# Two conventional FFN tiles put into the seven-product form at the start of the last block

## The chip, the cores and the metric

The kernel runs on one core of one Trainium2 chip. The metric is the time on the device in microseconds of one execution; lower is better. Before the change the median of three runs is 2493.28 us (2493.01 to 2493.83). The core has five engines with queues of their own: PE (TensorE, matrix products into PSUM), DVE (VectorE), ACT (ScalarE), POOL (GpSimd) and SP (SyncE, which here issues the DMAs). PEld in the profile is PE's loading of the stationary operand.

## The reference

Two pre-norm residual layers over a sequence of 1024 tokens, `D_MODEL` 1024, all in float32. The first has a Mamba-2 mixer, the second a Conformer convolution module; each mixer is followed by a SwiGLU feed-forward network (FFN) with `D_FF` 2816, that is 22 tiles of 128; a final RMSNorm ends the stack. What matters here is the second layer's FFN and the end:

```
def swiglu_ffn(u, w_gate, w_up, w_down):
    return (jax.nn.silu(u @ w_gate) * (u @ w_up)) @ w_down
...
        h = h + swiglu_ffn(rmsnorm(h, ffn_norm[i]), ffn_w_gate[i], ffn_w_up[i], ffn_w_down[i])
    return rmsnorm(h, final_norm)
```

## The kernel before

**Data.** The tokens lie in two blocks of 512 (block 0 and block 1). Activations are kept transposed: `h` has eight tiles of 128 features by 512 tokens for each block. Float32 accuracy comes from splitting each operand into an upper and a lower part (`split`, line 233: ACT copies the upper part, line 234, and DVE subtracts, line 235), and from three matmuls for each product: low by high, high by low, high by high (`gemm`, line 255).

**The FFN** of a block takes its 22 tiles in parts. For each part the gate and up products fill `hid`, and then eight output products (`dn`, line 977), one for each 128 output features, add the part's share to `h` (line 985). A conventional tile (`gu`, line 938) takes 24 matmuls of 512 columns for gate and 24 for up; its weights are split from `wst` into `whi` and `wlo`.

**The seven-product form** (`seven`, line 832) computes two neighbouring tiles at once by Strassen's scheme in Winograd's variant: the two tiles, the two halves of the features and the two halves (256 tokens) of the block make a 2 by 2 product of blocks that takes seven products instead of eight. Each product is 12 matmuls of 256 columns (line 881). It needs sums of the weights (`sums`, lines 850 to 852, on DVE), splits of the weights (`wa`, `wb`, `wc`) and readbacks of single products (lines 892 to 917). Gate and up of a pair are two such halves. On the other side it needs sums of the normalized input u: `sums_u` (line 783), whose three steps make t2 (`first`, lines 811 to 813 and a split), n3 and t4 (`second`, line 819 and two splits), and one operand written over a part of u (`last`, line 825). For block 1 of the last layer `norm_u` (line 324, `whole=True`) also leaves the unsplit u in `ru`, from which these sums start.

**The order.** Work is cut into units, and `run` makes a list `q` of them. Each unit's instructions get their priority from their place in the list; the scheduler below the kernel then sets each engine's own order from the priorities and what is ready in its reckoning. `chain7` (line 1009 on) strings the seven-product units of several parts together and puts one output product behind at least `gap` of them, from `lag` units after the part before is done; the last part's output products end the chain. So the first part of a chain has none of its own chain between its products. If the first part is conventional (a list of units, not of dictionaries), its units come first. Fetches, weight sums and weight splits are put ahead by `emit`: `pre` (line 921) gives how many us ahead of its unit each is to come, in times that the kernel reckons itself (`MM`, `MH`), and they get a priority earlier by `BOOST`. `put` and `at` insert units at given positions of a list, negative ones counted from its end.

**The place of the change.** At the end of `run` the last layer's block 0 runs tiles 12 to 21 in the seven-product form, with block 1's norm (`n1`) inserted near its end: five units, before the last ten to five units of the chain. The last eight units of that chain are the output products of block 0's last part of six tiles. Then comes block 1: tiles 0 and 1 conventional, then parts of 6, 6, 4 and 4 tiles in the seven-product form; the sums of u stand after the first, second and fourth conventional unit, and the final norm of block 0 (`f0`: one unit, then four that scale and store) after the second and third. The last part (tiles 18 to 21) has its output products in halves of 256 tokens, between which the final norm of block 1 runs (`f1`, `f2`).

Of the kernel before, what the change touches and what calls it, by code (L numbers as in the profile page):

```python
# [73 lines left out]
class Unit:  # L74
# [3 lines left out]
    def __init__(self, run, load=None, t=0.0, pre=()):  # L78
        self.run, self.load, self.t, self.pre, self.then = run, load, t, pre, None


def weave(main, fill):

    out, n, m, j = [], len(main), len(fill), 0
    for i, f in enumerate(main):
        out.append(f)
        want = (i + 1) * m // n
        out += fill[j:want]
        j = want
    return out  # L90


def put(q, *at):

    out = []
    for i in range(len(q) + 1):
        for k, units in at:
            if (k if k >= 0 else len(q) + k) == i:
                out += units
        out += q[i:i + 1]  # L100
    return out


def at(units, places):

    return [(p, units[i:i + 1] if i < len(places) - 1 else units[i:]) for i, p in enumerate(places)]


class Trunk:
# [405 lines left out]
    def in_proj(self, i, u=None, fac=None):  # L515
# [12 lines left out]
        def run(n):  # L528
# [9 lines left out]
            else:  # L538
# [3 lines left out]
                self.nc.scalar.activation(s, acc, AF.Tanh, scale=0.5)  # L542
                self.nc.vector.scalar_tensor_tensor(s, s, 1.0, acc, op0=ALU.add, op1=ALU.mult)
        units = [Unit(lambda n=n: run(n), lambda n=n: load(n)) for n in range(10)]
        if u is not None:
            self.W_in = W
# [649 lines left out]
    def run(self):  # L1196
        nc = self.nc
        self.h = {0: [], 1: []}
        self.U, self.UB, self.TU, self.TB, self.RU, self.sums, self.LU, self.LB = ({} for _ in range(8))
        self.whole = set()  # L1200
        self.ci, self.co = [], {0: [], 1: []}
        call = lambda f, *a: Unit(lambda: f(*a))
        self.consts()
        self.mixer_setup()
        fac = self.small.new("fac")
        raw = []
        dt = self.dt_path(0, raw, fac)
        r3, ip = self.in_proj(0, raw, fac)
        self.banks(mm=(0, 1, 2, 3, 4, 5), ss=(6, 7))
        self.warm(WARM)  # L1210
        products, rb = self.begin(raw, dt[0].load)
        r3[0].load()
        r3[0].load = None
        nu = self.norm_u(0, "ssm_norm", 0, fac, (0, 1, 3, 5, 7))
        q = [products] + nu[:2] + [call(self.halves, fac)] + nu[2:] + r3 + [call(lambda: self.big.drop(*rb))]
        q += dt[1:2] + [call(self.selects)] + dt[2:] + ip[:NR]
        q += [call(lambda: self.small.drop(fac)), call(lambda: self.banks(mm=(0, 1, 2, 3), ss=(4, 5, 6, 7)))] + ip[NR:]
        q += [call(self.load_x, 1)]
        for i in range(8):
            wo = self.w_out(i - 1) if i else []  # L1220
            post = []
            if i == 3:
                dtp = self.dt_path(1)
                ip = self.in_proj(4)
                n1 = self.norm_u(1, "ssm_norm")
                fill = [self.drop_u(0)] + put(wo, *at(n1, (0, 2, 3, 4, 6))) + dtp[:1] + ip[:1] + dtp[1:2] + ip[1:]
                post = dtp[2:]
            elif i < 7:
                ip = self.in_proj(i + 1)
                fill = ip[:3] + wo + ip[3:]  # L1230
                if i == 2:
                    fill = put(fill, *at(self.x_sums(1), range(1, 17, 2)))
            else:
                ag, ad = self.ffn(0, 18, 4, [0])
                fill = [self.drop_u(1)] + put(wo, *at(self.norm_u(0, "ffn_norm"), (2, 4, 5, 6, 8))) + ag[:6]
            q += weave(self.ssd(i), fill) + post
        q += [Unit(lambda: (self.big.drop(*self.mix_bigs), self.half.drop(*self.c_er, self.c_xt))), call(self.phase, 8)]
        fast = lambda *a, **k: self.ffn(*a, fast=True, **k)
        su = self.sums_u(0)
        q += ag[6:] + put(weave(self.w_out(7), ad), *at(su, (1, 3, 5, 8, 16)))  # L1240
        n1 = self.norm_u(1, "ffn_norm")
        c = self.chain7(fast(0, 0, 6, [0]), fast(0, 6, 6, [0]), fast(0, 12, 6, [0], [0]), free=0, hold=0)
        q += [call(self.phase7)] + put(c, *at(n1, (-10, -8, -7, -6, -5))) + [call(self.phase, 8)]
        n0 = self.norm_u(0, "cv_norm")
        p1, cv = self.pw1(0), self.conv31(0, 1000)
        c = self.chain(self.ffn(0, 10, 6, [1]), self.ffn(0, 16, 6, [1]))
        q += put(c[:4], *at(n0, (0, 1))) + [call(self.phase, 6, nc.gpsimd)]
        for j in range(8):
            q += p1[2 * j:2 * j + 2] + (cv[j:j + 1] if j < 4 else [])
        ln, p2 = self.cnorm(0), self.pw2(0)  # L1250
        q += cv[4:] + put(c[4:], *at(ln, (-11, -10, -9, -7, -5, -4, -3, -2)))
        q += [call(self.phase, 8)]
        q += put(p2, *at(self.sums_u(1, True), (2, 3, 4, 5, 6)))
        n0 = self.norm_u(0, "ffn_norm", 8)
        c = self.chain7(fast(0, 0, 4, [1]), fast(0, 4, 6, [1], [1]), free=1, hold=0)
        q += [call(self.phase7)] + put(c, *at(n0, (-10, -8, -7, -6, -5))) + [call(self.phase, 8)]
        n1 = self.norm_u(1, "cv_norm")
        p1, cv = self.pw1(1), self.conv31(1, 1200)
        c = self.chain(self.ffn(1, 0, 6, [0]), self.ffn(1, 6, 6, [0]))
        q += put(c[:4], *at(n1, (0, 1))) + [call(self.phase, 6, nc.gpsimd)]  # L1260
        for j in range(8):
            q += p1[2 * j:2 * j + 2] + (cv[j:j + 1] if j < 4 else [])
        ln, p2 = self.cnorm(1), self.pw2(1)
        q += cv[4:] + put(c[4:], *at(ln, (-11, -10, -9, -7, -5, -4, -3, -2)))
        q += [call(self.phase, 8)]
        self.whole = {1}
        q += put(p2, *at(self.sums_u(0, True), (2, 3, 4, 5, 6)))
        n1 = self.norm_u(1, "ffn_norm", 8, whole=True)
        c = self.chain7(fast(1, 12, 4, [0]), fast(1, 16, 6, [0], [0]), free=0, hold=0)
        q += [call(self.phase7)] + put(c, *at(n1, (-10, -8, -7, -6, -5)))  # L1270
        f0, f1, f2 = self.final(0), self.final(1, (0,)), self.final(1, (HT,))
        c = self.chain7(self.ffn(1, 0, 2, [1]), fast(1, 2, 6, [1]), fast(1, 8, 6, [1]), fast(1, 14, 4, [1]),
                        fast(1, 18, 4, [1], [1], True), free=1, hold=4)
        q += put(c, *at(self.sums_u(1), (1, 2, 4)), (2, f0[:1]), (3, f0[1:]), *at(f1, (-7, -5, -4, -3, -2))) + f2
        self.emit(q)

    def phase7(self):
# [100 lines left out]
```

## Time and profile before

| | |
|---|---|
| median of three runs | 2493.28 us |
| the profiled execution, its time | 2493.91 us |
| its span, first to last instruction | 2492.2 us |
| mean granted TensorE clock | 0.997 |
| block 1's norm, first to last DVE operation | 2103.3 to 2129.3 us |
| block 1's first conventional matmul | 2137.5 us |
| its first seven-product matmul | 2160.2 us |

Times in the views count from the start of the span. A row of the timeline gives start, duration, engine, line, operation, what is written from what (tile names without buffer numbers), shape, a count where equal neighbours are merged, and in brackets how long the engine was idle before and what ended that. A row of the stretches gives the stretch, its length, and for each engine its busy time and number of instructions, then the granted clock and the DMA figures. Matmuls overlap, so their durations are longer than the time from one start to the next.

### The profile page before, as it was taken

How to read it: one execution, taken by the hardware profiler on the slowest of the kernel's cores; microseconds unless marked ns; L12 is line 12 of the kernel's file. 1: busy time of each engine (PE TensorE's matmuls, PEld its weight loads, DVE VectorE, ACT ScalarE, POOL GpSimd, SP SyncE). 2: the span in 40 equal slices, each digit the busy share in tenths (PEclk: the TensorE clock that was granted, in tenths of full speed). 3: DMA queues.
4: the chain of work that ended last, by engine and by line, in shares of the span. 5: the costliest groups of instructions: out<-in, count | busy, mean ns of one | idle time of the engine just before them, and what ended most of it. 6: DMA issues, size and time to landing. Idle time of an engine off the chain costs nothing.

```text
span 2492.2 us, 35811 instructions
## 1 busy us (share of the span) xinstructions
PE 2471.1 (99%) x13752; PEld 2114.9 (85%) x13752; DVE 2052.9 (82%) x3030; ACT 1328.7 (53%) x2365; POOL 398.8 (16%) x406
## 2 busy tenths in 40 slices
PE   8999999999999999999999999999999999999998
PEld 6788887888887899998888789988887899899998
DVE  7988989878889886768799797778997977986675
ACT  5776776766667553545333455453335545554444
POOL 1212111112111000000444410004444100000000
PEclk9999999999999999999999999999999999999999
DMA  4222222222223332323223233232232323332322
GB/s 159 68 68 85 77 62 85 77 73 79 76 70 110 89 112 92 110 67 100 93 93 111 87 114 109 64 102 93 93 119 85 123 91 104 131 118 82 119 85 73
DMA packets 69516, 233.54 MB, mean 94 GB/s; under 512 B 7648, under 2 KB 11232, under 8 KB 61920
## 3 DMA queue, kind: packets, MB, share of 16 engines
q1 hardware_dynamic: 69344, 231.25, 28.5%
q8 instruction: 108, 1.77, 0.3%
q14 instruction: 64, 0.52, 0.1%
HBM read 227.02 MB, written 4.19 MB: 93 GB/s over the span
## 4 chain that ended last, share of the span: by engine, by line
PE 97%; DVE 2%; ACT 1%; issue 0%; DMA 0%; DVEq 0%; SPq 0%; ACTq 0%
PE p L259 68%; PE p L881 23%; PE p L712 1%; PE p L704 1%; PE p L667 1%; PE p L680 1%; PE p L681 1%; PE p L310 0%; PE p L647 0%; PE p L695 0%; DVE wlo L235 0%; PE p L408 0%; PE p L614 0%; PE p L615 0%; PE p L618 0%; DVE un_s L349 0%
## 5 line engine op out<-in xcount | busy, mean ns | idle before, releaser
L234 ACT ACTIVATE whi<-wst 128x512 fp32r<-128x512 f32 (+1 forms) x652 | 388.0, 597 | 689.3 <-PE p L259 577.9
L259 PE MATMUL p<-uhi_b,wlo 128*128 128x512 f32 x1344 | 533.7, 397 | 3.3 <-ACT uhi_b L234 1.8
L259 PE MATMUL p<-ulo_b,whi 128*128 128x512 f32 x1344 | 529.4, 394 | 1.6 <-POOL ulo_b L235 1.1
L259 PE MATMUL p<-uhi_b,whi 128*128 128x512 f32 x1344 | 530.5, 395 | 0.0
L259 PE MATMUL p<-hid_b,whi 128*128 128x512 f32 x1344 | 419.1, 394 | 0.2
L235 DVE TENSOR_TENSOR wlo<-wst,whi 128x512 fp32r<-128x512 f32 (+1 forms) x442 | 303.9, 690 | 123.5 <-ACT whi L234 120.2
L235 POOL TENSOR_TENSOR wlo<-wst,whi 128x512 fp32r<-128x512 f32 x208 | 256.4, 1236 | 724.3 <-ACT whi L234 720.9
L881 PE MATMUL p<-uhi_b,wh_b 128*128 128x256 f32 x1856 | 343.9, 280 | 0.0
L259 PEld LDWEIGHTS p<-uhi_b,wlo 128*128 128x128 f32 x1344 | 253.0, 188 | 62.4 <-ACT uhi_b L234 2.6
L259 PEld LDWEIGHTS p<-ulo_b,whi 128*128 128x128 f32 x1344 | 253.3, 188 | 61.9 <-POOL ulo_b L235 2.9
L259 PEld LDWEIGHTS p<-uhi_b,whi 128*128 128x128 f32 x1344 | 253.1, 188 | 59.2 <-issue 0.3
L259 PEld LDWEIGHTS p<-hid_b,whi 128*128 128x128 f32 x1344 | 251.9, 188 | 56.7 <-DVE hid_b L235 1.1
L881 PEld LDWEIGHTS p<-uhi_b,wh_b 128*128 128x128 f32 x1856 | 290.9, 188 | 3.2 <-ACT vw_s L908 0.8
L259 PE MATMUL p<-hid_b,wlo 128*128 128x512 f32 x672 | 264.3, 394 | 0.0
L881 PE MATMUL p<-ulo_b,wh_b 128*128 128x256 f32 x928 | 259.9, 280 | 0.0
L881 PE MATMUL p<-tu_b,wh_b 128*128 128x256 f32 x1392 | 183.2, 281 | 0.0
L881 PEld LDWEIGHTS p<-ulo_b,wh_b 128*128 128x128 f32 x928 | 174.6, 188 | 2.0
L234 ACT ACTIVATE wh_b<-ws_b 128x1024 fp32r<-128x1024 f32 x116 | 122.7, 1059 | 99.2 <-PE p L881 38.9
L881 PEld LDWEIGHTS p<-tu_b,wh_b 128*128 128x128 f32 x1392 | 173.6, 188 | 1.3
L1097 DVE SCALAR_TENSOR_TENSOR p<-ci_b,par,p 128x507 f32<-128x507 f32 (+29 forms) x240 | 160.3, 733 | 3.3 <-ACT p L1094 2.0
L235 DVE TENSOR_TENSOR wh_b<-ws_b,wh_b 128x1024 fp32r<-128x1024 f32 x116 | 141.1, 1221 | 25.6 <-ACT wh_b L234 25.3
L1099 DVE SCALAR_TENSOR_TENSOR p<-ci_b,par,p 128x512 f32<-128x512 f32 x232 | 158.1, 749 | 1.9 <-ACT p L1094 1.4
(282 smaller groups left out, 4027.1 us busy)
## 6 DMA issues: line engine op xcount, KB each, us to landing
wq_b<-w_gu SPq DMA_DIRECT2D x58, 1024.0 KB, 4.8
wst<-w_in SPq DMA_DIRECT2D x77, 512.0 KB, 3.5
wst<-w_dn SPq DMA_DIRECT2D x88, 384.0 KB, 3.1
wst<-w_gu SPq DMA_DIRECT2D x60, 512.0 KB, 3.5
wst<-w_pw SPq DMA_DIRECT2D x48, 512.0 KB, 3.5
wst<-w_out SPq DMA_DIRECT2D x64, 256.0 KB, 2.6
wst<-w_dn SPq DMA_DIRECT2D x40, 256.0 KB, 2.7
h<-xT SPq DMA_DIRECT2D x8, 512.0 KB, 8.8
```

What stands on the lines that cost most here:

```text
L234: self.nc.scalar.activation(hi, src, AF.Copy)
L235: (eng or self.nc.vector).tensor_tensor(lo, src, hi.bitcast(F32), ALU.subtract)
L259: self.nc.tensor.matmul(acc, a, b, start=n == 0, stop=n == tot - 1)
L667: nc.tensor.transpose(xt[:, zs(j)], self.XS[i][:, j, zs(z)], self.ident)
L680: nc.tensor.matmul(sg, self.gtr, aml, start=True, stop=False)
L681: nc.tensor.matmul(sg, self.gtr, amh, start=False, stop=True)
L704: nc.tensor.matmul(O[:, zs(j)], H[:, zs(j)], CT[:, zs(z)], start=True, stop=True)
L712: nc.tensor.matmul(Y[po:po + 64, zs(hh // 2)], self.XDT[z % 2][:, hh * 64:(hh + 1) * 64], E[:, zs(r)], start=True, stop=True)
L881: nc.tensor.matmul(to, x, y, start=n == 0 and not more, stop=n == 11, skip_group_check=True)
L1097: nc.vector.scalar_tensor_tensor(acc[:, s:], x[:, HALO:TW - s], w(s), acc[:, s:], op0=ALU.mult, op1=ALU.add)
L1099: nc.vector.scalar_tensor_tensor(acc if s < 30 else c, x[:, HALO - s:TW - s], w(s), acc, op0=ALU.mult, op1=ALU.add)
```

## The change

Block 1 of the last layer takes all 22 tiles in the seven-product form, in parts of 6, 6, 6 and 4. The three units of `sums_u(1)` move out of block 1's chain into the end of block 0's chain, before the last four, three and two units, among block 0's last output products; the units of block 1's norm after its first move up by one place each. The final norm of block 0 keeps its positions (after the second and the third unit) in block 1's chain, whose units are other ones now. The last part of four tiles is as before; the part ahead of it has six tiles instead of four.

```diff
-        q += [call(self.phase7)] + put(c, *at(n1, (-10, -8, -7, -6, -5)))
+        su = self.sums_u(1)
+        q += [call(self.phase7)] + put(c, *at(n1, (-10, -9, -8, -7, -6)), *at(su, (-4, -3, -2)))
         f0, f1, f2 = self.final(0), self.final(1, (0,)), self.final(1, (HT,))
-        c = self.chain7(self.ffn(1, 0, 2, [1]), fast(1, 2, 6, [1]), fast(1, 8, 6, [1]), fast(1, 14, 4, [1]),
+        c = self.chain7(fast(1, 0, 6, [1]), fast(1, 6, 6, [1]), fast(1, 12, 6, [1]),
                         fast(1, 18, 4, [1], [1], True), free=1, hold=4)
-        q += put(c, *at(self.sums_u(1), (1, 2, 4)), (2, f0[:1]), (3, f0[1:]), *at(f1, (-7, -5, -4, -3, -2))) + f2
+        q += put(c, (2, f0[:1]), (3, f0[1:]), *at(f1, (-7, -5, -4, -3, -2))) + f2
```

## The prediction

> **What bounds the kernel now.** I read the page first (busy shares, chain of work that ended last), then a table of stretches around the place that changes, then the timeline of PE and of DVE there.
>
> ```profile
> span 2492.2 us, 35811 instructions
> ...
> PE 2471.1 (99%) x13752; PEld 2114.9 (85%) x13752; DVE 2052.9 (82%) x3030; ACT 1328.7 (53%) x2365; POOL 398.8 (16%) x406
> ...
> PE 97%; DVE 2%; ACT 1%; issue 0%; DMA 0%; DVEq 0%; SPq 0%; ACTq 0%
> ```
>
> PE sets the end over nearly the whole span: removing PE work gains its own time, if nothing else comes late. What could come late is named by the stretches. Columns: stretch, length, then busy time (and instructions) of PE, PEld, DVE, ACT, POOL, then granted clock, DMA share and GB/s.
>
> ```profile
> 2090.00:2100.00 10.00, 10.00 (x87) 10.00 (x87) 3.10 (x5) 3.77 (x7) 0.00 (x0) 1.00 0.13 39
> 2103.30:2137.50 34.20, 34.20 (x152) 27.66 (x152) 33.08 (x54) 18.50 (x35) 0.00 (x0) 1.00 0.47 152
> 2137.50:2159.80 22.30, 22.30 (x98) 18.11 (x97) 21.80 (x29) 18.07 (x25) 0.00 (x0) 1.00 0.14 42
> 2159.80:2211.00 51.20, 51.20 (x385) 48.62 (x384) 49.75 (x73) 27.06 (x44) 0.00 (x0) 1.00 0.44 152
> 2211.00:2480.00 269.00, 269.00 (x1912) 252.34 (x1911) 190.20 (x279) 126.72 (x207) 0.00 (x0) 1.00 0.28 93
> ```
>
> The second stretch is the output products of block 0's last part, the third the two conventional tiles that are to go, the fourth the first seven-product tiles. PE has no gap in them; but DVE is busy 33.08 of 34.20, 21.80 of 22.30 and 49.75 of 51.20 us. From 2103 to 2211 DVE has 3 us to spare in 108. Whether the change gains is decided there.
>
> **What PE saves.**
>
> ```profile
> 2137.53 0.40 PE L259 MATMUL p<-uhi_b,wlo 128*128 128x512 f32 x1
> 2154.17 0.40 PE L310 MATMUL p<-suml_s,onesr 128*128 128x512 f32 x1
> 2154.40 0.39 PE L310 MATMUL p<-sumh_s,onesr 128*128 128x512 f32 x1
> 2160.18 0.28 PE L881 MATMUL p<-uhi_b,wh_b 128*128 128x256 f32 x1
> 2005.99 1.58 PE L881 MATMUL p<-tu_b,wh_b 128*128 128x256 f32 x12
> 2007.40 0.28 PE L881 MATMUL p<-uhi_b,wh_b 128*128 128x256 f32 x1
> ```
>
> The conventional tiles take 2160.18 - 2137.53 = 22.65 us; two matmuls in it are block 0's final norm (0.23 each, from one start to the next), so their 96 matmuls take 22.19. As one seven-product pair they are 14 products of 12 matmuls; a product takes 2007.40 - 2005.99 = 1.41, together 19.74. PE saves 2.45 us. The output products keep their matmuls (22 tiles by three by eight, regrouped). Eight `h += acc` on DVE disappear (40 become 32), as do eight small weight loads in w_dn; they lie after 2160 where PE does not wait, so I count them nothing. Bytes stay; four loads of 512 KB become two of 1024 KB.
>
> **What DVE must do, and by when.** Prices are taken from one start to the next in a stretch without gaps:
>
> ```profile
> 2151.86 1.22 DVE L235 TENSOR_TENSOR wh_b<-wq_b,wh_b 128x1024 fp32r<-128x1024 f32 x1
> 2153.00 0.41 DVE L235 TENSOR_TENSOR wlo<-wst,whi 128x256 fp32r<-128x256 f32 x1
> 2153.33 2.35 DVE L235 TENSOR_TENSOR wh_b<-ws_b,wh_b 128x1024 fp32r<-128x1024 f32 x2
> 2155.60 0.68 DVE L235 TENSOR_TENSOR wlo<-wq_b,whi 128x512 fp32r<-128x512 f32 x1
> 2156.20 1.22 DVE L235 TENSOR_TENSOR wh_b<-wq_b,wh_b 128x1024 fp32r<-128x1024 f32 x1
> 2105.32 0.95 DVE L967 TENSOR_TENSOR hx_x<-hx_x,hx_x 128x768 f32<-128x768 f32 x1
> 2106.19 0.69 DVE L317 SCALAR_TENSOR_TENSOR p<-p,rstd_s 128x512 f32<-128x512 f32 x1
> 2162.33 5.35 DVE L1189 SCALAR_TENSOR_TENSOR h<-h,par,p 128x512 f32<-128x512 f32 x8
> 2167.60 0.68 DVE L950 TENSOR_TENSOR sg_s<-sg_s,p 128x512 f32<-128x512 f32 x1
> ```
>
> 1024 columns 1.14, 768 columns 0.87, 512 columns 0.60, 256 columns 0.33; the eight scalar_tensor_tensor 5.27 / 8 = 0.66 each. So a gate or up half of a pair costs: weight sums (lines 850 to 852) 1.14 + 0.60 + 0.60 = 2.34, splits a11/a12, s2/s3, s1/s4 1.14 each and a22 0.60.
>
> Where does DVE stand when PE ends block 0?
>
> ```profile
> 2103.32 0.69 DVE L315 SCALAR_TENSOR_TENSOR p<-p,rstd_s 128x512 f32<-128x512 f32 x1
> 2128.61 0.69 DVE L235 TENSOR_TENSOR ulo_b<-ru_b,uhi_b 128x512 fp32r<-128x512 f32 x1
> 2136.07 1.22 DVE L812 TENSOR_TENSOR ru_b<-ru_b,ru_b 128x1024 f32<-128x1024 f32 x1
> 2139.65 1.22 DVE L813 SCALAR_TENSOR_TENSOR ru_b<-ru_b,ru_b 128x1024 f32<-128x1024 f32 x1
> 2140.78 0.68 DVE L283 TENSOR_TENSOR ssum_s<-ssum_s,sq_s 128x512 f32<-128x512 f32 x1
> 2160.25 1.23 DVE L235 TENSOR_TENSOR ulo_b<-ru_b,uhi_b 128x1024 fp32r<-128x1024 f32 x1
> ```
>
> Block 1's norm begins on DVE at 2103.3 and ends at 2129.3; of the sums of u only two of eight wide operations are done by T0 = 2137.5, the last at 2161.5. In the old order that was early enough: the seven products began at T0 + 22.7. In the new order they begin at T0.
>
> Demand counted from 2103.3, in the order in which products need it. Up to the third product (p6, needs t2 and s2): end of block 0's last pair 0.33 + 0.87 + 1.14 = 2.3; three rstd steps 1.9; norm 8 x (0.66 + 0.60) = 10.1; down weights 6 x (0.60 + 0.33) + 0.33 = 5.9; eight adds to h 4.8; seven additions of squares 4.2; lines 811 to 813 and the t2 split 4 x 1.14 = 4.6; weight sums and two splits 4.6. Sum 38.4. DVE has 34.2 until T0 and 2.8 for two products, 37.0: **1.4 us late**. (The old order's part of this, without the last 7.6 us and with three conventional splits of 0.60, is 32.6; the stretch shows 33.08.)
>
> Up to the up half's p5 (the twelfth product, due at 34.2 + 11 x 1.41 = 49.7): n3, t4 and the last split 4 x 1.14 = 4.6; the gate half's s1/s4 and a22 1.7; the up half 2.34 + 3.42 + 0.60 = 6.3; four readbacks of products into hx 4 x 0.33 = 1.3; the split for the final norm 0.6. Sum 38.4 + 14.5 = 52.9: **3.2 late**.
>
> Then the final norm of block 0, which the queue still places after the second and third unit of this chain, now two products instead of two 5.5 us units: 1.9 + 5.3 = 7.2. In the rows above its eight operations run in one piece and line 950 waits behind them, so they are taken ahead of younger work. Next gate half: a11/a12, sums, s2/s3 4.6 and a readback 0.3. Sum 65.0 for its p6, the sixteenth product, due at 34.2 + 15 x 1.41 = 55.3: **9.7 late**. Later DVE needs about 17 of each 19.7 us, so it falls no further behind. Nothing can cover on PE: block 0's output products are over, and block 1 has none until its first six tiles end, whereas before the small part's output products stood between the first products. Everything behind the late product waits in PE's queue. Block 0's output DMAs move forward on SP's queue with the norm; weights are fetched 12 us ahead of use by the queue's own reckoning (line 921), so I price that at nothing; with that cover gone, a load would be late by as much as DVE is, which is already in the sum. ACT makes the upper half of each split and was busy 18.07 of 22.30 us in the stretch that goes; the added pair gives it no more than DVE has, so it follows DVE.
>
> So the sums will not run beside block 0's output products: DVE is full there with the norm. The net is -2.45 + 9.7 = +7.3 us. The profiled execution took 2493.91 us (span 2492.2); the runs' median, 2493.28, is 0.63 lower. From it: **2500.6 us**.
>
> **Rivals.** *DVE keeps up (not slower).* Before 2103.3 DVE is mostly idle (3.10 of 10 us busy from 2090). The norm waits for two matmuls with ones at 2100.6, whose inputs are older:
>
> ```profile
> 2083.16 0.68 DVE L235 TENSOR_TENSOR suml_s<-ssum_s,sumh_s 128x512 fp32r<-128x512 f32 x1
> 2100.82 0.40 PE L310 MATMUL p<-sumh_s,onesr 128*128 128x512 f32 x1
> 2102.54 0.69 ACT L314 ACTIVATE rstd_s<-p,eps 128x512 f32<-128x512 f32 x1
> ```
>
> The change places the norm one unit earlier. If that moved those matmuls to 2091 or before, DVE would gain the 9.7 us that it lacks, and only PE's 2.45 would be left: 2490.8. Against it: one product is 1.41 us, and the matmuls already ran ahead of their place.
>
> *The final norm comes late.* If the order lets all weight work pass it, only 3.2 us are lost: 2493.28 - 2.45 + 3.2 = 2494.0. For it: it needs block 0's last squares, which finish after T0. Against: the uninterrupted eight above.
>
> *The accumulators add to it.* A third half reuses the first half's two banks, and its second product (fourteenth, due at 34.2 + 13 x 1.41 = 52.5) needs line 917 to have read the old one; if that waits behind all 65.0 us of older and prefetched work, PE pauses 12.5: 2503.3. A pause can cost clock too:
>
> ```profile
> 60.00:70.00 10.00, 5.25 (x19) 3.81 (x20) 9.35 (x15) 8.60 (x21) 4.79 (x7) 0.70 0.28 100
> 65.04 0.80 PE L680 MATMUL p<-am_b,sr_b 128*128 128x512 f32 x1 [3.12 <-ACT am_b L663]
> 70.08 0.63 PE L259 MATMUL p<-uhi_b,whi 128*128 128x512 f32 x1
> 70.51 0.58 PE L259 MATMUL p<-uhi_b,wlo 128*128 128x512 f32 x1
> ```
>
> After a pause of 3.12 us the stretch has clock 0.70 and matmuls start 0.43 apart instead of 0.23; eight such are 1.6 us. I take nothing for it in the sum, since DVE delivers an operand every 1 to 3 us, and 1.6 at the range's end: 2504.9. The Trainium skill ("TensorE: Matmul & The Clock Gate", Part 1, "What's actually happening") says the clock halves after an idle window of about 3.4 us and returns after as much busy time. By that rule one pause as long as the eight operations would cost about 1.7 us once (an estimate from the page); the row above agrees in size.
>
> **How the numbers follow.** Pause 7.5 to 11.3 us (2498.3 to 2502.1): 0.46. Accumulators or clock on top: 0.18. Final norm late, wholly or partly (2493.5 to 2498.3): 0.22. DVE keeps up (near 2490.8): 0.11. Something gained besides, below 2488.3: 0.03. About 0.2%, 5 us, is what a measurement can tell from no change. Slower 0.64, same 0.33, faster 0.03. The range, 2493.5 to 2504.9, leaves out DVE keeping up and the far ends.
>
> **What would show it.** Right: PE less than fully busy in the 25 us after T0, its idle time ended by DVE (tu, wh, hx) or by ACT halves of those splits; line 825's split ending 5 us or more after T0; DVE full from 2103 to beyond 2190; products 1.41 apart once the lead is back. Wrong: the norm's first row well before 2103, the final norm's eight rows after 2175, or another engine or a DMA ending PE's idle time.

## The result and the profile after

The kernel after takes 2504.96 us (median of six runs, 2503.75 to 2506.17), the kernel before 2493.86 us beside it: 11.1 us slower, ratio 1.0045 with a 95% interval of 1.0035 to 1.0055. The profiled execution took 2505.70 us. Its page has PE's and DVE's sums nearly as before; the chain that ended last has a little less of PE and more of DVE:

```profile
span 2504.0 us, 35932 instructions
...
PE 2472.7 (99%) x13824; PEld 2119.9 (85%) x13824; DVE 2058.3 (82%) x3033; ACT 1334.2 (53%) x2370; POOL 399.7 (16%) x406
...
PE 94%; DVE 3%; ACT 1%; DMA 0%; issue 0%; POOL 0%; DVEq 0%; SPq 0%; ACTq 0%
```

PE is busy about as long as before in a longer span: it idles 2504.0 - 2472.7 = 31.3 us instead of 2492.2 - 2471.1 = 21.1. The stretches show where (columns as in the prediction):

```profile
2130.00:2140.00 10.00, 10.00 (x52) 8.27 (x51) 10.00 (x13) 6.43 (x10) 0.00 (x0) 1.00 0.37 109
2140.00:2150.00 10.00, 4.68 (x34) 4.04 (x33) 10.00 (x12) 5.12 (x8) 0.00 (x0) 0.93 0.09 35
2150.00:2160.00 10.00, 8.65 (x56) 8.57 (x56) 10.00 (x14) 5.93 (x9) 0.00 (x0) 0.73 0.24 83
2160.00:2170.00 10.00, 10.00 (x85) 9.80 (x84) 9.23 (x16) 8.05 (x11) 0.00 (x0) 1.00 0.42 152
2170.00:2180.00 10.00, 7.80 (x65) 7.42 (x64) 10.00 (x15) 4.75 (x7) 0.00 (x0) 1.00 0.54 194
```

Block 1's first seven-product matmul starts at T0 = 2138.06. Behind it PE is busy 4.68 of 10 us while DVE is busy for all ten, then PE runs below full clock, then it falls short once more from 2170 to 2180. The timeline of PE names what it waited for (rows left out are marked by dots):

```profile
2138.06 0.38 PE L881 MATMUL p<-uhi_b,wh_b 128*128 128x256 f32 x1
...
2142.76 1.62 PE L881 MATMUL p<-tu_b,wh_b 128*128 128x256 f32 x12 [1.59 <-DVE wh_b L235]
2147.36 0.35 PE L881 MATMUL p<-uhi_b,wh_b 128*128 128x256 f32 x1 [2.98 <-DVE wh_b L235]
...
2151.35 0.58 PE L881 MATMUL p<-uhi_b,wh_b 128*128 128x256 f32 x1 [2.09 <-DVE wh_b L235]
...
2152.58 0.63 PE L881 MATMUL p<-uhi_b,wh_b 128*128 128x256 f32 x2
2153.01 0.41 PE L881 MATMUL p<-ulo_b,wh_b 128*128 128x256 f32 x1
...
2157.05 0.40 PE L881 MATMUL p<-uhi_b,wh_b 128*128 128x256 f32 x2
2157.29 0.28 PE L881 MATMUL p<-ulo_b,wh_b 128*128 128x256 f32 x1
...
2169.62 1.57 PE L881 MATMUL p<-tu_b,wh_b 128*128 128x256 f32 x12
2172.41 0.36 PE L881 MATMUL p<-uhi_b,wh_b 128*128 128x256 f32 x1 [1.22 <-DVE wh_b L235]
...
2176.46 1.68 PE L881 MATMUL p<-tu_b,wh_b 128*128 128x256 f32 x12 [0.98 <-DVE hx_x L897]
...
2480.08 5.94 PE L259 MATMUL p<-hid_b,wdn_b 128*128 128x256 f32 x48 [0.61 <-DVE wdn_b L235]
```

There are five pauses in 40 us, all ended by DVE. Counted from one matmul's start to the next, less its usual distance, they are 1.76, 3.14, 2.39, 1.38 and 1.14 us, together 9.8. The two pairs of rows in the middle show the clock: a row of two matmuls of 256 columns starts 2153.01 - 2152.58 = 0.43 us before the next one, and 0.24 us a little later. Some 23 matmuls between 2148 and 2155 start so slowly; that is about 2.1 us more. The last row is a pause of 0.8 us among the very last output products.

DVE's rows in the same stretch:

```profile
2103.99 0.69 DVE L315 SCALAR_TENSOR_TENSOR p<-p,rstd_s 128x512 f32<-128x512 f32 x1
...
2125.63 0.68 DVE L235 TENSOR_TENSOR ulo_b<-ru_b,uhi_b 128x512 fp32r<-128x512 f32 x1
...
2134.45 1.21 DVE L235 TENSOR_TENSOR tu_b<-ru_b,tu_b 128x1024 fp32r<-128x1024 f32 x1
...
2141.40 1.21 DVE L235 TENSOR_TENSOR wh_b<-ws_b,wh_b 128x1024 fp32r<-128x1024 f32 x1
...
2144.87 1.21 DVE L235 TENSOR_TENSOR ulo_b<-ru_b,uhi_b 128x1024 fp32r<-128x1024 f32 x1
2146.01 1.21 DVE L235 TENSOR_TENSOR wh_b<-ws_b,wh_b 128x1024 fp32r<-128x1024 f32 x1
...
2150.08 1.21 DVE L235 TENSOR_TENSOR wh_b<-wq_b,wh_b 128x1024 fp32r<-128x1024 f32 x1
...
2161.56 0.70 DVE L315 SCALAR_TENSOR_TENSOR p<-p,rstd_s 128x512 f32<-128x512 f32 x1 [0.52 <-ACT rstd_s L314]
2162.51 1.23 DVE L235 TENSOR_TENSOR wh_b<-ws_b,wh_b 128x1024 fp32r<-128x1024 f32 x1 [0.25 <-ACT wh_b L234]
...
2165.79 5.35 DVE L1189 SCALAR_TENSOR_TENSOR h<-h,par,p 128x512 f32<-128x512 f32 x8
2171.05 1.22 DVE L235 TENSOR_TENSOR wh_b<-ws_b,wh_b 128x1024 fp32r<-128x1024 f32 x1
...
2175.99 0.41 DVE L897 TENSOR_TENSOR hx_x<-vw_s,p 128x256 f32<-128x256 f32 x1
```

Block 1's norm starts at 2104 as before, its last split is at 2125.6, the sums of u follow and end with line 825's split at 2144.87 + 1.21 = 2146.1, 8.0 us after T0. Each of PE's first three pauses ends just behind one wh split: 2141.40 + 1.21 = 2142.6, 2146.01 + 1.21 = 2147.2, 2150.08 + 1.21 = 2151.3. The eight uninterrupted operations of block 0's final norm (5.35 us) precede the split that ends the fourth (2171.05 + 1.22 = 2172.3), and the fifth ends with a readback, line 897 (2176.4). From T0 to there DVE idles 0.8 us, in the two rows that show it.

### The profile page after: what moved, and what is told of

It reads as the page before. It is cut to its first block, busy times and chain, and to the rows that moved or that the text cites. A ratio compares the mean times of both kernels' runs of the same rounds, so it can differ in the third digit from the quotient of the medians.

```text
span 2504.0 us, 35932 instructions
## 1 busy us (share of the span) xinstructions
PE 2472.7 (99%) x13824; PEld 2119.9 (85%) x13824; DVE 2058.3 (82%) x3033; ACT 1334.2 (53%) x2370; POOL 399.7 (16%) x406
## 4 chain that ended last, share of the span: by engine, by line
PE 94%; DVE 3%; ACT 1%; DMA 0%; issue 0%; POOL 0%; DVEq 0%; SPq 0%; ACTq 0%
PE p L259 65%; PE p L881 23%; PE p L712 1%; PE p L704 1%; PE p L667 1%; PE p L680 1%; PE p L681 1%; DVE wlo L235 0%; PE p L310 0%; DMA wst<-w_dn 0%; PE p L647 0%; PE p L695 0%; DVE wh_b L235 0%; PE p L408 0%; PE p L614 0%
## 5 line engine op out<-in xcount | busy, mean ns | idle before, releaser
L259 PE MATMUL p<-uhi_b,wlo 128*128 128x512 f32 x1312 | 521.5, 398 | 3.7 <-DVE sf_b L503 2.0
L259 PE MATMUL p<-ulo_b,whi 128*128 128x512 f32 x1312 | 517.4, 394 | 1.4 <-POOL ulo_b L235 1.1
L259 PE MATMUL p<-uhi_b,whi 128*128 128x512 f32 x1312 | 518.4, 395 | 0.0
L881 PE MATMUL p<-uhi_b,wh_b 128*128 128x256 f32 x1920 | 357.6, 281 | 6.3 <-DVE wh_b L235 6.3
L881 PEld LDWEIGHTS p<-uhi_b,wh_b 128*128 128x128 f32 x1920 | 302.2, 189 | 10.1 <-issue 3.2
L259 PEld LDWEIGHTS p<-ulo_b,whi 128*128 128x128 f32 x1312 | 247.5, 189 | 59.5 <-POOL ulo_b L235 1.9
L881 PE MATMUL p<-ulo_b,wh_b 128*128 128x256 f32 x960 | 269.9, 281 | 0.0
L881 PE MATMUL p<-tu_b,wh_b 128*128 128x256 f32 x1440 | 189.8, 281 | 2.6 <-DVE wh_b L235 1.6
L881 PEld LDWEIGHTS p<-tu_b,wh_b 128*128 128x128 f32 x1440 | 179.7, 189 | 4.1 <-ACT sq_s L272 1.8
L881 PEld LDWEIGHTS p<-ulo_b,wh_b 128*128 128x128 f32 x960 | 181.6, 189 | 1.7
```

What stands on the lines that cost most here:

```text
L259: self.nc.tensor.matmul(acc, a, b, start=n == 0, stop=n == tot - 1)
L881: nc.tensor.matmul(to, x, y, start=n == 0 and not more, stop=n == 11, skip_group_check=True)
```

## The experiments

Two theories stood at the start. **A**: DVE's queue has a fixed order and is full from the norm's start at 2104 on, so the sums of u and the first weights come late; this can be cured by moving DVE work, and only so. **B**, the forecast's own shares: most of the loss (6.5 of 9.7 us) is the final norm of block 0. Further rivals belong to single runs and are lettered in the expectations. Each ratio is against the kernel before, run beside it on the same chip.

### e1: block 0's final norm later

```diff
-        q += put(c, (2, f0[:1]), (3, f0[1:]), *at(f1, (-7, -5, -4, -3, -2))) + f2
+        q += put(c, (44, f0[:1]), (46, f0[1:]), *at(f1, (-7, -5, -4, -3, -2))) + f2
```

> Block 0's final norm moves to the 44th and 46th place of block 1's chain, among the output products of its first part; all else as in the changed kernel (11.1 us slower than before in the runs on record). Theory A, a queue on DVE in which each pause is priced where it stands: of the five pauses of the changed kernel only the two at 2171 and 2175 (1.38 + 1.14 us) belong to the final norm, so this kernel is 2.5 us faster than the changed one, 8.6 us slower than before, and the first three pauses stay. Theory B, the budget as predicted: 6.5 of 9.7 us of pause belong to the final norm, so it is 6.5 us faster than the changed one, 4.6 us slower than before.

Measured: 2501.64 us, ratio 1.0030 (1.0019 to 1.0042). The pauses at 2172 and 2176 are gone; of the first three 1.76, 3.16 and 2.02 us remain, and the clock still falls:

```profile
2140.00:2150.00 10.00, 4.67 (x31) 4.03 (x29) 10.00 (x13) 5.06 (x8) 0.00 (x0) 0.89 0.06 25
2150.00:2160.00 10.00, 9.01 (x62) 9.02 (x63) 8.65 (x12) 4.76 (x7) 0.00 (x0) 0.77 0.09 13
```

This kernel is 7.7 us over its own before instead of 11.1. So the final norm is worth 3.4 us, nearer to A's 2.5 than to B's 6.5: B falls, and two thirds of the loss stay without it.

### e2: the last output products' weights split on POOL

POOL is free in this stretch. It takes the splits of block 0's last down weights from DVE (about 6 us). The edit holds from there on, so block 1's down weights are split on POOL too.

```diff
-        q += [call(self.phase7)] + put(c, *at(n1, (-10, -9, -8, -7, -6)), *at(su, (-4, -3, -2)))
+        q += [call(self.phase7), call(self.pool_weights)] + put(c, *at(n1, (-10, -9, -8, -7, -6)), *at(su, (-4, -3, -2)))
...
+    def pool_weights(self):
+        self.weng = self.nc.gpsimd
```

> The lower parts of the output products' weights are subtracted on POOL instead of DVE in the last layer's seven-product stage of both blocks; sums of u and order of the list as in the changed kernel. Theory A (DVE's backlog when block 0's products end): DVE is relieved of 6 x 0.93 + 0.33 = 5.9 us before block 1 begins, so the 7.3 us of pauses before the final norm shrink to about 1.4, no pause is long enough to lower the clock (another 2.3 us), and the kernel is 7 to 8 us faster than the changed one, 3 to 4 us slower than before. Rival C (the sums stand too late in the list, and DVE's load does not matter): no change, 11 us slower than before. Rival D (POOL's accesses slow DVE): DVE's 512-column subtractions last clearly over 0.69 us and less than half of the gain appears.

Measured: 2508.72 us, ratio 1.0060 (1.0047 to 1.0074), slower still. DVE's, POOL's and PE's timelines show why:

```profile
2125.84 1.21 DVE L811 TENSOR_TENSOR ru_b<-ru_b 128x1024 f32<-128x1024 f32 x1
2126.97 0.68 DVE L283 TENSOR_TENSOR ssum_s<-ssum_s,sq_s 128x512 f32<-128x512 f32 x1
2127.57 2.31 DVE L812 TENSOR_TENSOR ru_b<-ru_b,ru_b 128x1024 f32<-128x1024 f32 x1
...
2127.18 3.30 POOL L235 TENSOR_TENSOR wlo<-wst,whi 128x512 fp32r<-128x512 f32 x2 [2.41 <-ACT whi L234]
...
2135.66 0.50 PE L259 MATMUL p<-hid_b,wlo 128*128 128x512 f32 x1 [2.38 <-POOL wlo L235]
```

Line 811 runs while POOL is idle and takes 1.21 us; line 812, of the same size, starts while POOL is at work and takes 2.31. POOL's splits are slower too. Grouped by shape, from 2104 to 2140 in e2 and then over the whole kernel before (mean ns behind the comma):

```profile
L235 POOL TENSOR_TENSOR wlo<-wst,whi 128x512 fp32r<-128x512 f32 x6 | 10.7, 1775 | 12.8 <-ACT whi L234 12.8
L235 POOL TENSOR_TENSOR wlo<-wst,whi 128x256 fp32r<-128x256 f32 x7 | 7.8, 1109 | 6.5 <-ACT whi L234 6.3
```

```profile
L235 POOL TENSOR_TENSOR wlo<-wst,whi 128x512 fp32r<-128x512 f32 x176 | 232.1, 1319 | 712.2 <-ACT whi L234 708.8 <-issue 1.6 <-DMA wst<-w_gu 1.5
L235 POOL TENSOR_TENSOR wlo<-wst,whi 128x256 fp32r<-128x256 f32 x32 | 25.0, 782 | 12.1 <-ACT whi L234 12.1
```

The Trainium skill ("SBUF — State Buffer", "SBUF: two separate sides") says that a DVE operation with two SBUF inputs and a GpSimd operation that reads SBUF hold their shared pair of ports in turn, each for its whole length. The rows agree: the row of POOL merges a split of 512 columns with one of 256, the first of which ends at 2128.8 in the trace, and line 812 ends at 2129.9, 1.1 us later, as if it had begun only then. Line 851, 512 columns, takes 1.75 us beside a later split of POOL instead of 0.68. So POOL relieves DVE of 0.60 us for each 512-column split and takes much of it back (line 812 alone 1.1 us), and PE now waits for POOL's slower splits: 2.38 us in the row above, and 1.39 us again in the last part. Rival D holds.

### e3: matmuls that keep PE busy

```diff
-        q += put(c, (2, f0[:1]), (3, f0[1:]), *at(f1, (-7, -5, -4, -3, -2))) + f2
+        q += put(c, (2, f0[:1]), (3, [call(self.fill, 18)] + f0[1:]), *at(f1, (-7, -5, -4, -3, -2))) + f2
...
+    def fill(self, n):
+        acc = self.bank2()
+        for _ in range(n):
+            self.nc.tensor.matmul(acc, self.onesr, self.U[1][4][0], start=True, stop=True)
```

> 18 matmuls of 512 columns whose result nobody uses are put behind block 1's third product; the scheduler sets 6 before that product and 12 behind it, where the changed kernel pauses 1.8 and 3.1 us. Theory A: the pauses stay, but PE is not idle in them, so the clock stays at 1.00 in 2150 to 2160 instead of 0.73, and the kernel is about 2.3 us faster than the changed one, 8.8 us slower than before. Rival: the slow matmuls from 2148.6 to 2155 have another cause than the pauses, or cost nothing since DVE would have been late anyway; then no gain, 11 us slower than before or more.

Measured: 2506.92 us, ratio 1.0049 (1.0036 to 1.0062). In the profiled execution, which took 2503.86, the clock stayed full through the pauses:

```profile
2140.00:2150.00 10.00, 7.49 (x42) 6.19 (x42) 10.00 (x12) 5.61 (x8) 0.00 (x0) 1.00 0.00 0
2150.00:2160.00 10.00, 9.82 (x81) 9.74 (x82) 10.00 (x16) 7.93 (x13) 0.00 (x0) 1.00 0.31 107
```

That execution is 1.8 us under the profiled one of the kernel after, but the median is 2 us above. The two traces can be laid side by side from T0 on, the first row here:

```profile
2136.89 0.39 PE L881 MATMUL p<-uhi_b,wh_b 128*128 128x256 f32 x1
...
2170.28 0.36 PE L881 MATMUL p<-uhi_b,wh_b 128*128 128x256 f32 x1 [2.07 <-DVE wh_b L235]
```

T0 is 1.2 us earlier here, ahead of all added matmuls, so that part of the 1.8 us is not theirs. The product behind the fourth pause starts 33.4 us after T0, in the kernel after 2172.41 - 2138.06 = 34.4: only 1.0 us sooner, though the clock stayed full. PE comes earlier and waits longer for the same split, 2.07 us instead of 1.22. So in these two executions a full clock is worth about 1.0 us, since DVE is late in any case; the median does not confirm even that.

### e4: the moves of the sums of u and of the norm, in the kernel before

```diff
+        su = self.sums_u(1)
-        q += [call(self.phase7)] + put(c, *at(n1, (-10, -8, -7, -6, -5)))
+        q += [call(self.phase7)] + put(c, *at(n1, (-10, -9, -8, -7, -6)), *at(su[:2], (-4, -3)))
...
-        q += put(c, *at(self.sums_u(1), (1, 2, 4)), (2, f0[:1]), (3, f0[1:]), *at(f1, (-7, -5, -4, -3, -2))) + f2
+        q += put(c, (4, su[2:]), (2, f0[:1]), (3, f0[1:]), *at(f1, (-7, -5, -4, -3, -2))) + f2
```

The two conventional tiles stay, so nothing needs the sums early.

> The kernel before, with one part of the change alone: the first two steps of the sums of u and the norm's units take the new places beside block 0's output products; the two conventional tiles stay, and the sums' last step stays behind them, since it overwrites what they read. Theory A: the conventional tiles still hide the backlog, so the time is that of the kernel before, within 1 us, with PE without pauses. Rival E (the moved sums delay the output products' own DVE work): 2 us or more slower than before, with PE pausing before 2138.

Measured: 2499.78 us, ratio 1.0023 (1.0014 to 1.0032): 5.8 us lost with no product waiting for a sum. The trace has one pause of 4.0 us, and a granted clock of 0.83 in the ten us from 2140 on:

```profile
2140.43 0.50 PE L259 MATMUL p<-uhi_b,wlo 128*128 128x512 f32 x1 [3.85 <-DVE h L985]
...
2138.55 1.23 DVE L235 TENSOR_TENSOR tu_b<-ru_b,tu_b 128x1024 fp32r<-128x1024 f32 x1
2139.70 1.88 DVE L985 TENSOR_TENSOR h<-h,p 128x512 f32<-128x512 f32 x3
```

Three additions to h wait behind the sums and then run in one piece, and PE's next matmul, the first of the conventional tiles, waits for the last of them. The sums had not been free where they were put: DVE does not idle there, so they push out something that PE needs. The theory as I had put it (the conventional tiles hide the backlog) was wrong here; the rival was right. The edit also moves the norm's last four units up by one place; the two moves were not tried apart.

### e5, e6, e7: the whole norm of block 1 earlier

Before 2103 DVE does idle. e5 is the kernel after with the norm moved there; e6 adds e1's edit and moves the sums too (the norm's last three units stand one place later than in e5); e7 is the kernel before with the early norm alone.

```diff
-        q += [call(self.phase7)] + put(c, *at(n1, (-10, -9, -8, -7, -6)), *at(su, (-4, -3, -2)))
+        q += [call(self.phase7)] + put(c, *at(n1, (-18, -16, -15, -13, -12)), *at(su, (-4, -3, -2)))
```

> The changed kernel with block 1's norm further ahead in block 0's chain (before its last 18, 16, 15, 13 and 12 units instead of 10 to 6); the sums of u and block 0's final norm stay where the change put them. DVE is idle for some 10 of the 20 us before 2103 in the kernel before and in the changed one. Theory A (the pauses are a shortage of DVE time between the norm's start and the first products): the norm's 12 us of DVE work move into that idle stretch, the three pauses before the final norm (7.3 us) and the clock loss (about 2) go, those at the final norm (2.5 us) may stay; 9 us faster than the changed kernel, 0 to 3 us slower than the kernel before. Rival C (the sums stand too late in the list, whatever DVE has to do): the pauses stay, 11 us slower than before. Rival F (the earlier norm delays the products that it now stands among): new pauses before 2103, gain below half.

> As the kernel with the early norm, and besides the sums of u before the last 8, 6 and 4 units, and block 0's final norm after the 44th and 46th unit of block 1's chain. Theory A: no pause is left at the start of block 1, and only PE's saving of 2.45 us remains, 2491.5 us, 2 to 2.5 us faster than the kernel before. Rival: the added order costs something at another place (the output products, the last part), and the time is that of the kernel before or more.

> Control: the kernel before with the norm of block 1 at the same early places, nothing else changed. Theory A: PE had no pause there, the two conventional tiles hid the backlog, so the time stays that of the kernel before within 0.7 us. If it is faster by 2 us or more, the early norm gains something by itself, and a gain of the two kernels above is not the tiles'.

Measured: e5 2502.84 us, ratio 1.0037 (1.0023 to 1.0051); e6 2499.28, ratio 1.0021 (1.0013 to 1.0030); e7 2498.31, ratio 1.0017 (1.0009 to 1.0026). In e5 PE no longer pauses at the start of block 1 (busy 10.00 of 10 from 2130 to 2160), but does so 30 us earlier:

```profile
2109.74 0.50 PE L259 MATMUL p<-hid_b,wlo 128*128 128x512 f32 x1 [1.64 <-DVE wlo L235]
2116.86 1.65 PE L259 MATMUL p<-hid_b,wlo 128*128 128x512 f32 x3 [2.67 <-ACT hid_b L234]
...
2165.08 1.69 PE L881 MATMUL p<-tu_b,wh_b 128*128 128x256 f32 x12 [2.05 <-DVE hx_x L897]
```

The norm's operations now stand ahead of the readbacks, line 967 and the split that make block 0's last hid, and the output products wait for these. In e7, where no change of the products is in play, this alone costs 4.6 us. Theory A missed in all three: e5 gained 2 us of its 9 on the kernel after, e6 came out at 2499.3 and not 2491.5, e7 not within 0.7 us of the kernel before. Rival F of e5 (gain below half) and the rival of e6 were right, but for the place: the new pauses lie behind 2103.

### e8, e9, e10: the norm parted

Now two of the norm's five units come early and three stay behind block 0's last hid (e8); or one and four (e9); in e10 the sums come a place earlier as well. All have e1's late final norm.

```diff
-        q += [call(self.phase7)] + put(c, *at(n1, (-10, -9, -8, -7, -6)), *at(su, (-4, -3, -2)))
+        q += [call(self.phase7)] + put(c, *at(n1, (-18, -16, -8, -7, -6)), *at(su, (-4, -3, -2)))
...
+        q += [call(self.phase7)] + put(c, *at(n1, (-18, -9, -8, -8, -8)), *at(su, (-4, -3, -2)))
...
+        q += [call(self.phase7)] + put(c, *at(n1, (-18, -16, -8, -8, -7)), *at(su, (-5, -4, -3)))
```

> The kernel after, with the first two units of block 1's norm 18 and 16 units before the end of block 0's chain (in the stretch before 2103 in which DVE still idles), its other three units behind block 0's last hid split (8, 7 and 6 before the end), the sums of u where the change has them, and the final norm of block 0 as late as in e1. Theory A (DVE's fixed queue is full from the norm's start on; only work moved into the idle stretch ahead of 2103, and nothing that block 0's last hid needs moved behind it, helps): the pauses near 2108 and 2114 stay under 1 us together, the 7.3 us at the start of block 1 fall to under 3, no pause at f0; about 2492 to 2495. Rival F (every operation of the norm ahead of block 0's last hid split delays it by its own length): pauses of 2 to 4 us near 2110, and 2496 to 2499.

> As e8, but only the first unit of the norm is early (18 units before the end); the other four stand 9, 8, 8 and 8 before the end. Theory A: no pause over 1 us near 2108 to 2114; what is left at the start of block 1 lies between e1's 6.9 us and e8's: 3 to 5 us; about 2494 to 2497. Rival F: as for e8, but only some 1 to 2 us near 2110, so that it comes out under e8.

> As e8, with the fourth and fifth unit of the norm one place earlier (8 and 7 before the end) and the sums of u at 5, 4 and 3 before the end instead of 4, 3 and 2. Theory A says that order alone can gain little more: in e8 DVE idles for only some 0.6 us between 2105 and 2140, so whatever comes earlier there pushes as much behind it; the sum of the pauses at the start of block 1 stays 2 to 4 us (e8: 0.6 + 2.0), and the time within 2 us of e8's, 2495 to 2498. Rival G (it is the order at the start of block 1 that costs, and the sums stand in the way of the weights' sums there): the pauses fall under 1 us and the clock stays full, 2492 to 2494, level with the kernel before.

Measured: e8 2496.63 us, ratio 1.0010 (1.0001 to 1.0019); e9 2500.66, ratio 1.0027 (1.0016 to 1.0037); e10 2495.10, ratio 1.0004 (0.9995 to 1.0013). In e8 no pause is left near 2110, and those at the start of block 1 are 0.64 and 1.97 us, 2.6 together, as theory A had it; the time is 1.6 us above its range and inside rival F's, whose pauses near 2110 are missing. Some of it is the clock (0.83 from 2140 to 2150):

```profile
2141.43 0.39 PE L881 MATMUL p<-uhi_b,wh_b 128*128 128x256 f32 x1 [0.47 <-DVE h L985]
2144.93 0.38 PE L881 MATMUL p<-uhi_b,wh_b 128*128 128x256 f32 x1 [1.81 <-DVE wh_b L235]
```

e9 missed both expectations. Its early unit did not bring the norm's first operations forward (line 315 is still at 2104), and four norm units close together hold back three additions to h, as in e4:

```profile
2122.62 0.80 PE L259 MATMUL p<-hid_b,wlo 128*128 128x512 f32 x1 [5.27 <-DVE h L985]
...
2121.88 1.88 DVE L985 TENSOR_TENSOR h<-h,p 128x512 f32<-128x512 f32 x3
```

In e10 a pause of 0.70 us (behind an addition to h) is left among block 0's output products, one of 1.38 us at the start of block 1, and that of the last part:

```profile
2134.38 0.50 PE L259 MATMUL p<-hid_b,wlo 128*128 128x512 f32 x1 [0.54 <-DVE h L985]
2144.30 0.38 PE L881 MATMUL p<-uhi_b,wh_b 128*128 128x256 f32 x1 [1.22 <-ACT vw_s L901]
...
2470.05 5.93 PE L259 MATMUL p<-hid_b,wdn_b 128*128 128x256 f32 x48 [0.64 <-DVE wdn_b L235]
```

It is level with the kernel before: 9.9 of the change's 11.1 us are had back by the order of the same operations alone (excess over its own before 1.17 us). For e10 the expectations had drawn a line between 2495 and 2494, and 2495.1 lies too near it to decide: the pauses (2.1 us ahead of the last part, 1.4 of it in block 1) are more than the rival's, but the clock stayed full (1.00 from 2130 on), as the rival had it.

### e11: smaller parts at the end

```diff
-        c = self.chain7(fast(1, 0, 6, [1]), fast(1, 6, 6, [1]), fast(1, 12, 6, [1]),
+        c = self.chain7(fast(1, 0, 6, [1]), fast(1, 6, 4, [1]), fast(1, 10, 4, [1]), fast(1, 14, 4, [1]),
```

> As e10, but block 1's 22 tiles in parts of 6, 4, 4, 4 and 4, so that the part ahead of the last has four tiles, as before the change (PE's matmuls are the same in number; DVE has eight additions to h more). Theory E (the 0.8 and 0.3 us near 2469 and 2484, which every kernel with parts of 6, 6, 6 and 4 has and no kernel with the old parts, come with the six-tile part ahead of the last): both go, the time falls by 0.5 to 1.3 us against e10, to 2493.8 to 2494.6. Rival H (they come from the last part alone, or from what the queues owe each other from earlier): they stay, and the time is 2495 or, with the additions to h, up to 2497.

Measured: 2494.37 us beside 2493.47 before, ratio 1.0004 (0.9995 to 1.0013). PE's timeline has no pause left behind 2182, so the 0.8 us at the end does come with the six-tile part ahead of the last one. The expectation's second pause, 0.3 us, is none: the step in question, between two rows of line 310, is 0.43 us in e10, in e11 and in the kernel before alike (there 2481.69 to 2482.12). In the time that gain cannot be told from e10: 0.90 us above its own before, against 1.17. What links the part's size to the late weights was not tried.

No version beat the kernel before; e10 and e11 are level with it.

## Why the prediction was wrong

The sign was right, and so was the reason for it: PE waits for a full DVE at the start of block 1. The size was not: +11.1 us measured against about +7.3 forecast. (Of the distance from 2500.6 to 2504.96 us, another 0.6 is the starting point: the kernel before took 2493.86 us beside the result, and the forecast starts from 2493.28.) Worked from the profiled executions:

| term | forecast, us | shown, us |
|---|---|---|
| profiled execution before | 2493.91 | 2493.91 |
| PE's work saved | -2.45 | -2.45, not measured by itself; seven-product matmuls keep their distance |
| T0 later in this execution (2138.06, 2137.53 before) | 0 | +0.5 |
| pauses behind T0 | +9.7 | +9.8 (1.76 + 3.14 + 2.39 + 1.38 + 1.14) |
| slow matmuls, by the clock | 0 | +2.1 |
| pause in the last part | 0 | +0.8 |
| not assigned | | +1.0 |
| sum | 2501.2 | 2505.7 |

The later T0 is not the change's: the norm's first row is later by as much (2103.99 against 2103.32), and e3, whose list is the same up to there, has T0 at 2136.89.

**What held.** Line 825's split ends 8.0 us after T0 (5 or more were named), DVE is full beyond 2190 but for 0.8 us, the five pauses are ended by DVE, and the norm did not start earlier than 2103. "So the sums will not run beside block 0's output products" held by half: four of their eight wide operations are done by T0, two before the change. "DVE keeps up" is refuted by the times; "the final norm comes late" by e1, which makes it late and takes 2501.6, not 2494.0.

**The step that failed: how late DVE makes PE.** The forecast priced three products, the third, the twelfth and the sixteenth, found 1.4, 3.2 and 9.7 us, and stopped: "Later DVE needs about 17 of each 19.7 us, so it falls no further behind." In the trace the product behind the fourth pause is PE's seventeenth. Without waiting it would start 16 x 1.41 us and the 0.46 us of the final norm's two matmuls after T0, that is 23.0; it starts 34.4 after T0, **11.3 us late**. The nineteenth, behind the fifth pause, starts 38.4 after T0 instead of 25.8, **12.6 us late**. DVE, which idles 0.8 us in all that time, releases both. So the term of 9.7 us measured 12.6, of which 9.8 were pauses, 2.1 slow matmuls, and 0.7 smaller delays. The order behind the sixteenth product was not as forecast: its split (2162.51) runs ahead of the final norm's eight operations and ends at 2163.7, and the eight hold up the next split (2171.05) instead; then weight sums and a split of the following half stand ahead of the readback (2175.99) that the nineteenth product waits for. This work was still to come when the forecast stopped.

**The clock, put at nothing.** "I take nothing for it in the sum, since DVE delivers an operand every 1 to 3 us." DVE did so (the pauses are 1.1 to 3.1 us), and the clock fell all the same: granted 0.93 and 0.73 in two stretches, about 2.1 us by the distance of the matmuls. The range's end had 1.6 for it. About half of it PE would otherwise have waited: with a full clock e3's trace has the seventeenth product 1.0 us sooner, not 2.1. The Trainium skill ("TensorE: Matmul & The Clock Gate", Part 1, "What's actually happening") speaks of an idle window of about 3.4 us; no pause here is that long, and the matmuls are slow from 2148.6 on, behind two pauses (1.6 and 3.0 us idle) with one product between them. Here the measurement decides.

**A term that was missing.** The end of the kernel: the part ahead of the last was regrouped from four tiles to six, which I noted only as fewer additions to h. It brought a pause of about 0.8 us, and e11 shows that it goes with that part.

**The pauses: the same sum by luck, and wrong shares.** The pauses add up to 9.8 us and the forecast said 9.7, but 2.8 us of the lateness passed in slow matmuls and smaller delays and not as pauses. The sixteenth product is itself about as late as forecast, 10.0 us (2169.62), but without a pause, and its split had been ready for 5.9 us: it only carries on what the first three pauses and the clock had cost. The shares show it too. The forecast had 3.2 us until the up half's p5 and 6.5 through the final norm; the profile has 7.3 and 2.5. The longest pauses are ahead of the fourth and the fifth product, gate's p5 and up's p1, which the forecast did not price. It counted products as the kernel's list has them (gate's p1, p2, p6, p7, p5, then up's p1); PE's order in the trace has gate's p5 fourth and up's p1 fifth, the rows at 2147.36 and 2151.35. DVE's work up to up's first split took from 2103.99 to 2150.08 + 1.21 = 2151.3, 47.3 us; PE would have been there after 2138.06 - 2103.99 + 4 x 1.41 = 39.7. That is 7.6 us late, and the first three pauses sum to 7.3. Counting by need would not have found this: gate's p5 needs 38.4 us and three operations of 1.14 (n3, the last split, s1/s4), 41.8 in all, and is due at 34.2 + 4 x 1.41 = 39.8 in the list, only 2.0 late. But DVE works by priority and not by need: additions to h, sums of squares and weight sums of the next half stood ahead of splits that PE was waiting for.

**Rivals in the range.** "The accumulators add to it" named line 917 of the third half; that wait is not among the pauses of the kernel after, but the fifth, 1.14 us, is for another readback, line 897. The additions to h matter in the same way: e4 and e9 pause 4.0 and 5.4 us for them.

What stays open: the clock's price in the median (e3), which of e4's two moves costs the 5.8 us, and whether e10 and e11 stand above the kernel before at all. They do by 1.2 and 0.9 us, with intervals that reach below it; PE's 2.45 us less work and their pauses of 2.9 and 2.3 us nearly cancel, and no run took these pauses away.

## What to carry to other kernels

A queue with a fixed order that is full passes no work for free: before moving operations into a stretch, count its idle time there, and name which operation they displace and which engine waits for it; in e4 the moves alone, with nothing waiting for the sums, cost 5.8 us. When lateness is worked out from a budget, price every product and not a few, go on until the backlog is gone, and take both orders from the trace, that in which the consumer asks and that in which the producer delivers; they decide where the pauses fall and so what an edit can return. And where pauses of one to three microseconds follow each other closely, price the clock too, but only for the part that the wait does not cover anyway.

## What the runs showed of the hardware

- Clock, two or more pauses: in the kernel after, 1.6 and 3.0 us idle with 1.5 us of matmuls between brought about half the matmul rate from 2148.6 on (0.21 us from start to start instead of 0.12); it lasted some 7 us, a third pause of 2.1 us among them, and then the full rate came back without any further change. e8's two pauses, 0.5 and 1.8 us within 4 us, gave 0.83 in its stretch; e10's, 0.5 and 1.2 us ten microseconds apart, gave 1.00, and so did e3's 2.1 and 1.0 us within 5 us.
- Clock, one pause: e3's 2.3 us gave 1.00, e4's 3.9 us 0.83 and e9's 5.3 us 0.66 in their stretches of ten. The runs show no simple rule for several short pauses.
- DVE beside POOL: the same 1024-column operation took 2.31 us instead of 1.21 when POOL was running a split, and POOL's splits of 512 columns took 1.78 us on average instead of 1.32, those of 256 columns 1.11 instead of 0.78.
